# Rooms for gathered cache rows and window keys in a pool that is opened earlier, and the first of them requested beside the prompt's attention

## The chip, the cores and the metric

The kernel runs on one core of one Trainium2 chip. The metric is the device time of one execution in microseconds. Three runs of the kernel before took 1896.36, 1897.3 and 1900.26 us; the median is 1897.3 us.

## The reference, cut to what matters

One step of a hybrid decoder is computed for a prompt group (1 x 1024 tokens) and a sample group (8 sequences x 4 new tokens, each with 2048 cached positions in pages, and 512 rows of window state). Both share all weights. In float32:

```
h = rms_norm(x, g_attn); q, kc, vc, ks, vs, kw, vw, gates, ... = split(h @ w_in)
kcmp, vcmp = compress(kc), compress(vc)     # gelu(flat(32 rows + pe) @ w1) @ w2, stride 16
pc = softmax(q kcmp + bias);  o_cmp = pc vcmp
imp = pc @ sel_map;  idx = top 16 of the 64-row blocks (first, current and previous always in)
o_slc = softmax(q ks[idx] + bias) vs[idx]
o_win = softmax(q kw + bias over the last 512) vw
a = g0 o_cmp + g1 o_slc + g2 o_win
x = x + (sig(ga) (a @ w_nsa_out) + sig(gb) (conv @ w_conv_out)) @ w_o;  x = x + relu(norm(x) @ w_up)^2 @ w_down
```

For the sample group kc, vc, ks and vs are the cached pages, found by a page table, followed by the new rows, and kw and vw are the window state followed by the new rows. The step also returns the window state moved on by four rows (s_wk, s_wv).

## The kernel before, in words

The kernel is unrolled Python for a tile framework. The author writes tiles, pools and instructions; a list scheduler that runs against a planned timeline (schedule_with_timeline_sim) then fixes the order on each engine and each queue. An instruction that is written earlier has the better priority; tc.high_priority lifts what is written in it by 500 places; issue_after(x) puts what follows behind x on its engine. A tile whose room was another tile's waits for that tile's last use. Pools are opened on the left or the right end of the memory, as a stack on each side. All matmuls on wide data are done in three passes of high and low halves (mm3, L214 to L216).

The stages in order: RMSNorm and projections; the conv mixer's inputs; gates, with the prompt's attention beside them (stages(), driven by keep_pace and advance, at high priority); the conv output (pool conv); the sample group; merge; MLP.

Around the change:
- At the end of the conv output the pools gt and unit are opened on the right. gt holds GB = 2 rooms gth of 8 KB a partition: the compression's raw cache rows of one sequence, gathered by POOL (gather, L640).
- Four single units (sample_unit, i = 0 to ATTEND = 3) compress the cached keys of sequences 0 to 3 while the rest of the prompt's attention runs: compress(...), then advance(STEP[i]). Then advance(100) writes what is left of the attention, the pools unit, pa (the attention's, with its output tile ot) and cTh are closed, and s1, u2 and w2 are opened, with new PSUM banks (SMP).
- From there pairs of sequences are compressed (pair_unit, i = 4, 6, ... 14: two pairs of keys, four of values, in three products n = 0, 1, 2). The product n = 0 uses summed weights w2 (printed w), eight tiles of 256 KB that load_w2 loads on SP (L494). After each product the loop takes SSTEP = 3, 3, 4 steps of probs.
- probs = sample_group() is a generator: the sample group's own attention, step by step. weights(grp) transposes the window keys of four sequences (tiles swn, SWB = 2 rooms of 2 KB, loaded on SP at L1155), stores the moved window state from them (keep_window, L1103 and L1104), forms logits (sn, sw), the choice of blocks (L1206 with the constant lt, loaded at L1123), and the logits over the gathered selection rows (tiles gk, GK = 4 rooms of 4 KB, gathered by POOL at L633, 512 KB each; transposed at L1129). values(grp) multiplies by gathered value rows (so, L1113). fetch() asks for the next of 32 gathers whenever a room was used.
- In the kernel before, the rooms gk and swn are in s1. Two next(probs) are written right after s1 is opened: they write the first four gathers, lt, the first two key loads and their stores. load_w2 follows, its last four loads put behind the second key load.
- SP's queue carries, in order, the attention's stores (L990), lt, two key loads, then w.

Of the kernel before, what the change touches and what calls it, by code (L numbers as in the profile page):

```python
# [11 lines left out]
F32 = mybir.dt.float32  # L12
# [29 lines left out]
SWB = 2  # L42
# [34 lines left out]
GK = 4  # L77
# [43 lines left out]
def tile_hybrid_step(ctx, tc, xp, xs, cck, ccv, csk, csv, swk, swv, sconv, ptab, g_attn, w_in,  # L121
# [33 lines left out]
    def f32(ap):  # L155
        return ap.bitcast(F32)
# [261 lines left out]
    for j in range(4):  # L418
# [8 lines left out]
        h = j // 2  # L427
# [55 lines left out]
                P.dma_start(w2_d[sums, lp], f32(z).rearrange("p x c -> p (x c)"))  # L483
        return out

    def load_w2(kv, behind=None):

        out = {}
        for lp in range(8):
            z = w2p.tile([128, 2, 256], F32R, name="w2", tag="w2", bufs=8)  # L490
            with ExitStack() as e:
                if behind is not None and lp >= 4:
                    e.enter_context(tc.issue_after(behind.ins))
                DMA.dma_start(f32(z).rearrange("p x c -> p (x c)"), w2_d[kv, lp])  # L494
            out[16 + lp] = (z[:, 0], z[:, 1])
        return out

    HT = dict(ct="tp", hid="hd")

# [128 lines left out]

    def gather_half(cache, b, q):

        g = s1.tile([128, 1024], F32, name="gk", tag="gk", bufs=GK)
        rows = cache[0].rearrange("n (c q l) h d -> (n c q) (l h d)", q=2, l=8)
        P.indirect_dma_start(out=g, out_offset=None, in_=rows,  # L633
                             in_offset=bass.IndirectOffsetOnAxis(ap=idx2[:, q, b:b + 1], axis=0))
        return g
# [479 lines left out]
                    e.enter_context(tc.issue_after(ins.ins))  # L1115

    new_rows = {}
    nat_in = []

    def sample_group():  # L1120

        lt = s1.tile([128, 900], BF16, name="lt", bufs=1)
        DMA.dma_start(lt, lt_in.to_broadcast([128, 900]))  # L1123
        qb = [qbd[:, b].rearrange("p h g t -> p (h g t)") for b in range(NB)]
# [9 lines left out]
        def window_values(pw, rows, bs, ow):  # L1134
            pt = flipped([pw[:, i * 128:(i + 1) * 128] for i in range(4)], S.copy)
            po3 = ps(HT["sx"], "sv")
            for j0 in (0, 2):
                nats = {}
                for j in (j0, j0 + 1):
                    nats[j] = s1.tile([128, 4, 128], F32, name="swn", tag="swn", bufs=SWB)  # L1140
                    DMA.dma_start(nats[j], swv[0, bs[j]].rearrange("(k p) h d -> p k (h d)", p=128))
                    keep_window(s_wv[0, bs[j]], nats[j])
                in_turn([(po3[rows[j], :128], pt[:, i * 128 + 32 * j:i * 128 + 32 * j + 32], nats[j][:, i, :], i == 0, i == 3)
                         for i in range(4) for j in (j0 + 1, j0)])
            V.tensor_copy(ow, po3[:, :128])

        def weights(grp):
# [3 lines left out]
            bs = [grp * 4 + j for j in range(4)]  # L1151
            kts = []
            for b in bs:
                nat = s1.tile([128, 4, 128], F32, name="swn", tag="swn", bufs=SWB)
                nat_in.append(DMA.dma_start(nat, swk[0, b].rearrange("(k p) h d -> p k (h d)", p=128)))  # L1155
                keep_window(s_wk[0, b], nat)
                kts.append(flipped([nat[:, k, :] for k in range(4)], S.copy))
                yield
            while ("k", bs[-1]) not in have:
# [89 lines left out]
        def values(grp, ow):  # L1249
            rows = [slice(32 * j, 32 * j + 32) for j in range(4)]  # L1250
            bs = [grp * 4 + j for j in range(4)]
            def weights_T(q, n):
                pl = s1.tile([128, 512], F32, name="skt", tag="skt", bufs=SKT)
                DMA.dma_start(pl[:, :n], sl_d[grp, q, :, :n])
                return pl

            for half in range(2):
                pl = [weights_T(2 * half + i, 512) for i in range(2)]
                oo = ps(HT["sx"], "so")
                for j0 in (0, 2):  # L1260
                    gs = {j: gathered.pop(0) for j in (j0, j0 + 1)}
                    in_turn([(oo[rows[j], :128], pl[i // 4][:, i % 4 * 128 + 32 * j:i % 4 * 128 + 32 * j + 32],
                              gs[j][:, i * 128:(i + 1) * 128], i == 0, i == 7) for i in range(8) for j in (j0 + 1, j0)])
                    for _ in gs:
                        fetch()
                    yield
                V.tensor_add(ow, ow, oo[:, :128])
            pl = weights_T(4, 256)
            vn = s1.tile([128, 4, 128], F32, name="vn", tag="swn", bufs=SWB)[:8]
            DMA.dma_start(vn[:4], s_sv[0, bs[0]:bs[0] + 4].rearrange("b t h d -> t b (h d)"))  # L1270
            DMA.dma_start(vn[4:], s_wv[0, bs[0]:bs[0] + 4, WIN - ST:].rearrange("b t h d -> t b (h d)"))
            while ("v", bs[-1]) not in have:
                yield
            oo = ps(HT["sx"], "so")
            back = list(enumerate(bs))[::-1]
            in_turn([(oo[rows[j], :128], pl[:127, rows[j]], vcN[:, b, :], True, False) for j, b in back] +
                    [(oo[rows[j], :128], pl[:8, 128 + 32 * j:160 + 32 * j], vn[:, j, :], False, True) for j, b in back])
            V.tensor_add(ow, ow, oo[:, :128])
            yield
            own = s1.tile([128, 2, 64], F32, name="own", tag="mx")  # L1280
            V.tensor_scalar(own[:, 0], ow[:, 0:64], cst[:, K_M0:K_M0 + 1], None, op0=OP.mult)
            V.scalar_tensor_tensor(own[:, 0], ow[:, 64:128], cst[:, K_M1:K_M1 + 1], own[:, 0], op0=OP.mult, op1=OP.add)
            V.tensor_copy(own[:, 1], own[:, 0])
            pt = ps(HT["sk"], "ownT")
            PE.transpose(pt[:, :128], own.rearrange("p e d -> p (e d)"), ident)
            ts = mp.tile([128, 4, 16], F32, name=f"ts{grp}")
            for e in range(2):
                ro_ = slice(e * 64, e * 64 + 64)
                V.tensor_copy(ts[ro_].rearrange("p k (b t) -> p k b t", t=4),
                              pt[ro_, :128].rearrange("p (b k e t) -> p e k b t", b=4, k=4, e=2)[:, e])  # L1290
            new_rows[grp] = ts
            yield

        wanted = [(c, grp * 4 + j, half) for c in (csk, csv) for grp in range(2) for half in range(2) for j in range(4)]
        gathered = []

        def fetch():
            if wanted:
                gathered.append(gather_half(*wanted.pop(0)))

        for _ in range(GK):
            fetch()
        ows = []
        for grp in range(2):
            ows.append((yield from weights(grp)))
# [54 lines left out]
    def load_aT(qi):  # L1360
# [3 lines left out]
        for k in range(0, 4, 2):  # L1364
            S.copy(aTh[:, k:k + 2, s], at[:, k:k + 2])
            V.tensor_sub(aTl[:, k:k + 2, s], at[:, k:k + 2], f32(aTh[:, k:k + 2, s]))

    for i in range(ATTEND + 1):
        compress(sample_unit("k", cck, i, w1), ("k", i))
        advance(STEP[i])  # L1370
# [5 lines left out]
    w2p = open_pool("w2", "right")  # L1376
    HT.update(ct="ct", hid="hid", sk="sk", sx="sx")
    open_psum(**SMP)
    for _ in range(2):
        next(probs)  # L1380

    w1.update(load_w2(0, nat_in[-1]))
    for i in range(ATTEND + 1, 2 * NB, 2):
        if i == NB:
            w2 = load_w2(1)
            w1 = load_w1(w1v, W1B) | w2
        kv, cache = (("k", cck), ("v", ccv))[i // NB]
        unit = pair_unit(kv, cache, i % NB, w1)
# [530 lines left out]
```

## Time and profile before

| | |
|---|---|
| median of 3 runs | 1897.3 us (1896.36 to 1900.26) |
| profiled execution, own time | 1900.52 us |
| its span, first to last instruction | 1898.7 us |
| mean granted TensorE clock | 0.986 of full speed |
| busy: PE, PEld, DVE | 97%, 91%, 60% |
| busy: ACT, POOL | 46%, 25% |
| DMA, mean over the span | 163 GB/s |

The profile is one execution on the chip. PE is TensorE's matmuls, PEld its weight loads, DVE is VectorE, ACT ScalarE, POOL GpSimd, SPq the queue of SyncE, which issues most DMAs. Lxxx is a line of the kernel before. out<-in are the program's names for tiles. In brackets stands the time for which the engine had nothing just before, and what ended that wait. A clock of 1.00 is 2.4 GHz, 0.50 is 1.2 GHz.

### The profile page before, as it was taken

The numbers are of one execution on the slowest core, as the hardware profiler recorded it, in microseconds if no ns is written. First come the engines' busy times: TensorE is split into PE (matmuls) and PEld (weight loads), VectorE is DVE, ScalarE is ACT, GpSimd is POOL, SyncE is SP. The second block draws the span as 40 slices with busy tenths as digits, with TensorE's granted clock in tenths as the row PEclk, the third lists the DMA queues.
The fourth block names the chain that finished last, engine by engine and source line by source line (L and its number), as shares of the span: only waits on it lengthen the run. The fifth ranks groups of instructions, "written<-read, shape, count | busy, mean of one in ns | idle before, by whom it ended". The sixth has DMA issues, their size and how long they took to land.

```text
span 1898.7 us, 34944 instructions
## 1 busy us (share of the span) xinstructions
PE 1838.9 (97%) x13124; PEld 1734.0 (91%) x13124; DVE 1130.0 (60%) x2367; ACT 877.0 (46%) x1947; POOL 474.0 (25%) x710
## 2 busy tenths in 40 slices
PE   9999999999999999979999999999999999999998
PEld 7999999999998989858889887889999999999998
DVE  6324532444445676648777643697667646767765
ACT  5213322655555555656766212554545444544343
POOL 3213323445344443433332420131111100000000
PEclk9999999999999999989999999999999999999999
DMA  6457525322225531145757743546756567855664
GB/s 211 128 149 167 168 67 144 100 67 72 62 67 175 190 136 54 49 154 190 237 180 254 261 141 129 150 136 234 245 191 210 205 219 244 262 186 165 185 200 150
DMA packets 234202, 310.08 MB, mean 163 GB/s; under 512 B 21110, under 2 KB 162055, under 8 KB 229937
## 3 DMA queue, kind: packets, MB, share of 16 engines
q1 hardware_dynamic: 218416, 236.00, 40.5%
q0 software_dynamic: 15616, 71.84, 10.7%
q8 instruction: 104, 1.70, 0.4%
q14 instruction: 66, 0.53, 0.1%
HBM read 224.88 MB, written 82.90 MB: 162 GB/s over the span
## 4 chain that ended last, share of the span: by engine, by line
PE 83%; DMA 6%; DVE 4%; issue 3%; ACT 2%; POOL 2%; SPq 1%; POOLq 0%; DVEq 0%; ACTq 0%
PE c L215 10%; PE c L214 10%; PE c L216 10%; PE PT L957 3%; PE ga L215 3%; PE ga L214 3%; PE ga L216 3%; PE pv L964 2%; PE hid L215 2%; PE hid L216 2%; PE hid L214 2%; PE pv L963 2%; PE qkv L216 1%; PE qkv L215 1%; PE qkv L214 1%
## 5 line engine op out<-in xcount | busy, mean ns | idle before, releaser
L214 PE MATMUL c<-ud,whd 128*128 128x264 f32 x768 | 217.4, 286 | 5.5 <-ACT whd L1704 4.4
L215 PE MATMUL c<-ud,whd 128*128 128x264 f32 x768 | 218.4, 286 | 0.0
L216 PE MATMUL c<-ud,whd 128*128 128x264 f32 x768 | 215.6, 285 | 0.0
L883 POOL TENSOR_SCALAR P<-P,st,gates 128x256 f32<-128x256 f32 (+4 forms) x272 | 150.2, 568 | 115.9 <-DVE st L879 84.6
L214 PEld LDWEIGHTS c<-ud,whd 128*128 128x128 f32 x768 | 145.1, 190 | 6.1 <-ACT whd L1704 4.9
L214 PE MATMUL c<-hBt,wuh 128*128 128x264 f32 x512 | 145.9, 285 | 3.0 <-ACT p L1590 3.0
L216 PE MATMUL c<-hBt,wul 128*128 128x264 f32 x512 | 146.1, 285 | 0.0
L215 PEld LDWEIGHTS c<-ud,whd 128*128 128x128 f32 x768 | 145.4, 189 | 0.0
L216 PEld LDWEIGHTS c<-ud,whd 128*128 128x128 f32 x768 | 143.7, 189 | 0.0
L961 DVE TENSOR_TENSOR ptl<-PT,pth 128x512 fp32r<-128x512 f32 (+1 forms) x148 | 99.5, 685 | 64.1 <-ACT pth L960 63.6
L1704 ACT CAST whd<-wrd 128x512 fp32r<-128x512 f32 x112 | 68.2, 621 | 130.8 <-issue 97.8
L214 PE MATMUL ga<-hTh,whu 128*128 128x384 f32 (+1 forms) x384 | 127.7, 333 | 0.0
L215 PE MATMUL ga<-hTl,whu 128*128 128x384 f32 (+1 forms) x384 | 126.3, 329 | 0.0
L216 PE MATMUL ga<-hTh,wlu 128*128 128x384 f32 (+1 forms) x384 | 125.9, 328 | 0.0
L237 POOL TENSOR_TENSOR wlu<-wru,whu 128x1024 fp32r<-128x1024 f32 x32 | 76.7, 2398 | 154.1 <-ACT whu L236 154.0
L1705 DVE TENSOR_TENSOR whd<-wrd,whd 128x512 fp32r<-128x512 f32 x112 | 76.0, 689 | 64.3 <-ACT whd L1704 64.3
L960 ACT CAST pth<-PT 128x512 fp32r<-128x512 f32 (+1 forms) x148 | 83.7, 588 | 61.0 <-PE PT L957 57.5
L215 PE MATMUL c<-h2r,wuh 128*128 128x264 f32 x384 | 109.8, 286 | 1.4 <-POOL h2r L1616 0.8
L957 PE MATMUL PT<-cst,P 128*128 128x128 f32 (+1 forms) x592 | 101.8, 277 | 0.2 <-DVE st L938 0.2
L214 PEld LDWEIGHTS c<-hBt,wuh 128*128 128x128 f32 x512 | 97.2, 190 | 3.2 <-ACT p L1590 3.2
L216 PEld LDWEIGHTS c<-hBt,wul 128*128 128x128 f32 x512 | 96.9, 189 | 0.0
L1625 POOL DMA_DIRECT2D u_d<-u x64 | 34.7, 543 | 248.7 <-ACT u L1623 240.8
(554 smaller groups left out, 5977.9 us busy)
## 6 DMA issues: line engine op xcount, KB each, us to landing
ur<-u_d SPq DMA_DIRECT2D x96, 264.0 KB
wru<-in_w_up SPq DMA_DIRECT2D x36, 512.0 KB
u_d<-u POOLq DMA_DIRECT2D x64, 264.0 KB, 3.8
wru<-in_w_in SPq DMA_DIRECT2D x32, 512.0 KB
wrd<-sd_d SPq DMA_DIRECT2D x64, 256.0 KB
h2r<-in_w_down SPq DMA_DIRECT2D x28, 512.0 KB
sd_d<-h2r POOLq DMA_DIRECT2D x14, 1024.0 KB, 5.3
wrd<-in_w_down SPq DMA_DIRECT2D x48, 256.0 KB
```

Source lines behind the costliest of these rows:

```text
L214: PE.matmul(out, wh, ah, start=first, stop=False)
L215: PE.matmul(out, wh, al, start=False, stop=False)
L216: PE.matmul(out, wl, ah, start=False, stop=last)
L237: (leng or P.tensor_sub)(l, raw, f32(h))
L883: P.tensor_scalar(p, p, self.st[:, br, 3, g:g + 1], gates[:, self.qi, 3 * hg + br:3 * hg + br + 1], op0=OP.mult, op1=OP.mult)
L957: PE.transpose(pt[:n, g * 128:(g + 1) * 128], pg[g], ident)
L960: S.copy(hi[:n], pt[:n])
L961: V.tensor_sub(lo[:n], pt[:n], f32(hi[:n]))
L963: PE.matmul(self.o, w, hi[:n], start=first and i == 0, stop=False)
L964: PE.matmul(self.o, w, lo[:n], start=False, stop=last and i == len(tiles) - 1)
L1704: S.copy(h, raw)
L1705: lows.append(V.tensor_sub(l, raw, f32(h)))
```

## The change

Three things change. The tiles gk, swn and vn are taken from gt in place of s1. The generator has a new first part, which writes the four first gathers and the first two key loads with their stores, and then yields; it is run once, before the four single units. The two steps behind the opening of s1 are dropped, load_w2 has no loads held back, and key loads written after it stand behind its last load. lt is now written at the first step inside the unit loop.

```diff
-    def load_w2(kv, behind=None):
+    def load_w2(kv):
...
-            with ExitStack() as e:
-                if behind is not None and lp >= 4:
-                    e.enter_context(tc.issue_after(behind.ins))
-                DMA.dma_start(f32(z).rearrange("p x c -> p (x c)"), w2_d[kv, lp])
+            ins = DMA.dma_start(f32(z).rearrange("p x c -> p (x c)"), w2_d[kv, lp])
             out[16 + lp] = (z[:, 0], z[:, 1])
-        return out
+        return out, ins
...
     def gather_half(cache, b, q):
-        g = s1.tile([128, 1024], F32, name="gk", tag="gk", bufs=GK)
+        g = gt.tile([128, 1024], F32, name="gk", tag="gk", bufs=GK)
...
+        def keys(b):
+            nat = gt.tile([128, 4, 128], F32, name="swn", tag="swn", bufs=SWB)
+            with ExitStack() as e:
+                if w2_in:
+                    e.enter_context(tc.issue_after(w2_in[0].ins))
+                DMA.dma_start(nat, swk[0, b].rearrange("(k p) h d -> p k (h d)", p=128))
+            keep_window(s_wk[0, b], nat)
+            return nat
+
+        for _ in range(GK):
+            fetch()
+        early = [keys(b) for b in range(SWB)]
+        yield
         lt = s1.tile([128, 900], BF16, name="lt", bufs=1)
         DMA.dma_start(lt, lt_in.to_broadcast([128, 900]))
...
-                    nats[j] = s1.tile([128, 4, 128], F32, name="swn", tag="swn", bufs=SWB)
+                    nats[j] = gt.tile([128, 4, 128], F32, name="swn", tag="swn", bufs=SWB)
...
-                nat = s1.tile([128, 4, 128], F32, name="swn", tag="swn", bufs=SWB)
-                nat_in.append(DMA.dma_start(nat, swk[0, b].rearrange("(k p) h d -> p k (h d)", p=128)))
-                keep_window(s_wk[0, b], nat)
+                nat = early.pop(0) if early else keys(b)
...
-        for _ in range(GK):
-            fetch()
         ows = []
...
+    next(probs)
     for i in range(ATTEND + 1):
         compress(sample_unit("k", cck, i, w1), ("k", i))
         advance(STEP[i])
...
-    for _ in range(2):
-        next(probs)
-
-    w1.update(load_w2(0, nat_in[-1]))
+    w2, ins = load_w2(0)
+    w1.update(w2)
+    w2_in.append(ins)
```

(wanted, gathered and fetch move up with the gathers; vn is taken from gt as well.)

## Rows read from the trace of the kernel before

**Rows 1.** Page, part 1: busy us of each engine (share of the span), instructions.

```profile
PE 1838.9 (97%) x13124; PEld 1734.0 (91%) x13124; DVE 1130.0 (60%) x2367; ACT 877.0 (46%) x1947; POOL 474.0 (25%) x710
```

**Rows 2.** PE in order of time at the hand-over: start, us, what [wait, releaser].

```profile
829.08 0.50 PE L964 MATMUL pv<-ptl,pvc 64*128 64x512 f32 x1
831.80 1.86 PE L674 MATMUL ct<-cst,gpr 128*128 128x128 f32 x8 [2.23 <-DVE gpr L653]
841.50 2.02 PE L1129 MATMUL skT<-cst,swn 128*128 128x128 f32 x8 [7.83 <-DMA swn<-in_state_win_k]
...
844.02 0.56 PE L214 MATMUL hid<-cth,w 128*128 128x256 f32 x1
```

**Rows 3.** Windows of 2 us: length, busy PE PEld DVE ACT POOL, PEclk, DMA, GB/s.

```profile
832.00:834.00 2.00, 1.66 (x8) 1.26 (x7) 0.08 (x1) 0.89 (x2) 0.87 (x2) 0.50 0.91 326
...
844.00:846.00 2.00, 2.00 (x13) 2.00 (x12) 0.00 (x0) 1.24 (x3) 0.00 (x0) 0.59 0.89 286
```

**Rows 4.** SP's queue in order of time at the hand-over: start, us, issue.

```profile
830.46 1.43 SPq L990 DMA_DIRECT2D aT_d<-ot  x2
836.27 0.34 SPq L1123 DMA_DIRECT2D lt<-in_lt  x1
836.66 0.98 SPq L1155 DMA_DIRECT2D swn<-in_state_win_k  x2
837.68 1.64 SPq L494 DMA_DIRECT2D w<-w_d  x3
```

**Rows 5.** Waits of SP's queue, 780 to 900: total us, times, longest.

```profile
SPq L1123 <- DMA aT_d<-ot: 4.2, 2, 4.0
```

**Rows 6.** POOL in order of time, at gt's opening and at the hand-over.

```profile
699.83 1.07 POOL L640 DMA_INDIRECT gth<-in_cache_cmp_k,idx  x1 [0.90 <-DVE ptl L961]
...
704.26 6.91 POOL L883 TENSOR_SCALAR P<-P,st,gates 128x384 f32<-128x384 f32 x12 [1.71 <-DVE st L879]
...
825.51 0.98 POOL L633 DMA_INDIRECT gk<-in_cache_slc_k,idx  x1 [0.16 <-issue]
```

**Rows 7.** VectorE in order of time at the hand-over.

```profile
835.08 0.69 DVE L697 TENSOR_TENSOR ctl<-xt,cth 128x512 fp32r<-128x512 f32 x1
```

**Rows 8.** Windows of 2 us around the second half's gathers.

```profile
880.00:882.00 2.00, 0.83 (x5) 0.61 (x5) 1.97 (x2) 1.99 (x4) 1.70 (x2) 1.00 0.92 334
882.00:884.00 2.00, 0.91 (x9) 0.42 (x8) 2.00 (x6) 2.00 (x5) 1.39 (x3) 0.79 1.03 311
884.00:886.00 2.00, 0.74 (x5) 0.77 (x5) 1.12 (x3) 0.23 (x1) 0.76 (x1) 0.50 1.02 397
```

**Rows 9.** POOL's groups of instructions, 690 to 832: busy us, mean ns.

```profile
L640 POOL DMA_INDIRECT gth<-in_cache_cmp_k,idx x6 | 6.0, 1002 | 2.7 <-DVE ptl L961 1.6 <-POOL gpr L649 0.8 <-DVE st L879 0.3
...
L633 POOL DMA_INDIRECT gk<-in_cache_slc_k,idx x4 | 3.8, 958 | 1.1 <-issue 1.1
```

**Rows 10.** Windows of 4 us where the compression of the sample group begins.

```profile
700.00:704.00 4.00, 2.89 (x16) 2.01 (x13) 3.84 (x17) 2.61 (x10) 1.89 (x2) 1.00 0.65 210
704.00:708.00 4.00, 2.83 (x18) 2.21 (x18) 2.55 (x10) 2.04 (x8) 3.73 (x6) 1.00 0.96 391
```

**Rows 11.** The tile gth: its gathers of values, ns min/median/max.

```profile
L640 POOL DMA_INDIRECT gth<-in_cache_cmp_v,idx x8: 938/1032/1957, 873.7 to 985.7; - x8
```

**Rows 12.** PE in order of time later: last early key transposes, end of the units.

```profile
863.55 0.60 PE L1129 MATMUL skT<-cst,swn 128*128 128x128 f32 x4
...
1051.07 1.16 PE L531 MATMUL kvc<-w2v,gx 128*127 128x64 f32 x8 [0.86 <-DVE gx L507]
...
1066.60 1.94 PE L1113 MATMUL so<-gk,skt 128*32 128x128 f32 x32 [1.20 <-DMA gk<-in_cache_slc_v,idx]
...
1071.27 1.08 PE L214 MATMUL na<-aTh,wnh 128*128 128x288 f32 x3 [0.83 <-ACT aTh L1424]
```

**Rows 13.** POOL in order of time at the end of the sample group.

```profile
1057.62 0.94 POOL L633 DMA_INDIRECT gk<-in_cache_slc_v,idx  x1 [0.30 <-issue]
```

**Rows 14.** The tile gk: idle us before its instructions by releaser, times.

```profile
  PE so L1113: 29.7, 6
```

More of the change, by code (lines that the diff above doesn't have):

```diff
@@ L1117, in tile_hybrid_step, with fetch @@
     new_rows = {}
-    nat_in = []
+    w2_in = []
     def sample_group():
+        wanted = [(c, grp * 4 + j, half) for c in (csk, csv) for grp in range(2) for half in range(2) for j in range(4)]
+        gathered = []
+        def fetch():
+            if wanted:
+                gathered.append(gather_half(*wanted.pop(0)))
+        def keys(b):
[10 more added lines that the diff above has]
+        yield
         lt = s1.tile([128, 900], BF16, name="lt", bufs=1)
@@ L1268, in values @@
             pl = weights_T(4, 256)
-            vn = s1.tile([128, 4, 128], F32, name="vn", tag="swn", bufs=SWB)[:8]
+            vn = gt.tile([128, 4, 128], F32, name="vn", tag="swn", bufs=SWB)[:8]
             DMA.dma_start(vn[:4], s_sv[0, bs[0]:bs[0] + 4].rearrange("b t h d -> t b (h d)"))
@@ L1292, in values @@
             yield
[L1294 to L1299, printed above, removed]
-        for _ in range(GK):
-            fetch()
         ows = []
@@ L1378, in tile_hybrid_step @@
     open_psum(**SMP)
-    for _ in range(2):
-        next(probs)
-    w1.update(load_w2(0, nat_in[-1]))
+    w2, ins = load_w2(0)
+    w1.update(w2)
+    w2_in.append(ins)
     for i in range(ATTEND + 1, 2 * NB, 2):
         if i == NB:
-            w2 = load_w2(1)
+            w2, _ = load_w2(1)
             w1 = load_w1(w1v, W1B) | w2
```

## The prediction

> **What bounds the kernel now.** I read the page's shares first: PE is busy 97% of the span [rows 1], so the whole kernel has some 60 us in which PE waits, and only work that is in PE's way counts. The reader should then go to the stretch that the change touches, the hand-over from the prompt's attention to the sample group. PE's own instructions in order of time [rows 2] show it: the last attention matmul starts at 829.08; eight transposes of compression rows follow after 2.23 us of waiting; then PE stands 7.83 us until 841.50, and what ends that wait is the load of a key row (swn); the first product with the summed weights (hid from w) starts at 844.02. The clock rows [rows 3] add the second half of the cost: the granted clock is 0.50 from 832 on and still 0.59 as a mean over 844 to 846, so the lower of its two levels (1.2 GHz) holds until about 845.6, after an engine that had nothing for 10 us.
>
> Why is the key row late? SP's queue [rows 4] answers: two stores of the attention's output at 830.46, then nothing until lt at 836.27, then two key loads at 836.66, then w. The waits of that queue [rows 5] say that lt stood up to 4.0 us for the landing of aT_d from ot. Everything behind lt stood with it. The gathered rows (gk), which the change also moves, were asked for at 825.51 [rows 6], when POOL had finished the last scaling of P; they are not what PE waits for here.
>
> **The change part by part.**
>
> *The key rows.* Two loads and their four keep_window stores go from behind lt to a place beside the attention, with room in gt. That takes the 7.83 us wait away. What is late next is the pair unit itself: its first lower half ctl starts at 835.08 and takes 0.69 [rows 7], so hid cannot start before 835.77; and its first weight tile w. In the new program load_w2 stands ahead of lt (lt is now asked for in the loop), so I take w to be first on SP behind the two stores, which end at 830.46 + 1.43 = 831.89, and to be issued at about 832.2. The nearest row for its flight is the first key load, issued at 836.66 and used at 841.50: 4.84 us with lt (128 x 900 bf16) ahead of it. So w is there at 837.0, against 844.02 now: **7.0 us**. The eight key transposes (2.02 us even at the low clock) fit into the 3.3 us between 833.7 and 837.0. Ends: 8.2 us if w comes earlier and ctl decides (844.02 less 835.77); 2.5 us if lt still stands ahead and w is issued at 836.66 as the keys were (844.02 less 841.5). I take 7.0, by the row of the same queue and size. "DMA: Bandwidth & Descriptors" of the Trainium skill, in its anatomy of one DMA, fits a transfer as 2.0 us plus its bytes at 436 GB/s; that estimate is 2.6 us for 256 KB, and by it w would land at 834.8 and the term would be 8.2. That fit is for GpSimd's path; the row, on SP's queue, is nearly twice as long.
>
> *The clock.* From 841.50 to about 845.6 PE works at half rate, which costs 4.1 / 2 = 2.1 us. In the new kernel PE still has 2.2 us without work before 831.8 and some 1 to 3 us before hid. Ends: 0 and 2.1 gained. I take 0: at 882 to 884 the clock fell with only about half of the stretch idle [rows 8].
>
> *The four gathers.* Each is one POOL instruction of 958 ns, 0.3 us apart: some 5.0 us of POOL's queue for four [rows 6, 9]. They go from 825.5, where POOL had nothing else (gain 0), to the opening of gt, ahead of the compression's first gathers, now at 699.83 [rows 6]. These 1 MB gathers then start and land up to 5.0 us later, and the scaling of P at 704.26 stands behind them on POOL. There PE is already short of work: 2.89 and 2.83 us busy in two 4 us stretches [rows 10], 28% idle, since the attention alone does not fill it. Ends of the loss: 0 (the gathers fit into the 0.9 us holes and PE's order is planned around them) and 8.3 us, worked out below. I take 28% of 5.0 = **1.4 us lost**, by the row of that stretch.
>
> The six gathers that ran beside the attention took 1002 ns each, four in the emptier stretch 958 [rows 9]: 4 x 0.044 = 0.2 us, hidden by POOL's slack. "DMA: Bandwidth & Descriptors" of the Trainium skill, in SWDGE vs HWDGE vs iDMA, speaks against this part: GpSimd writes a gather's descriptors into SBUF, and VectorE locks it out while it runs in its two-port mode. The longest gather of this trace, 1957 ns beside a busy VectorE [rows 11], bounds what that could do: 4 x 1.0 = 4.0 us on POOL, of which 28% would be another 1.1 us. The trace bears the small value out.
>
> *SP's new work beside the attention.* Two loads and four stores at 0.5 us (two loads take 0.98) [rows 4] are some 3 us of a queue that otherwise carries q loads and output stores there; a store that waits for its key row can hold the queue for the 4.84 us of such a load, with a q load behind it. I cost it at nothing, since a q tile has two buffers; if that cover is gone, the price is at most 4.8 us once.
>
> *Moved steps.* The sample group gets two steps fewer before the unit loop. From the first hid at 844.02 [rows 2] to the last kvc at 1051.07 [rows 12] six units of ten steps take 207 us, 3.45 us a step, so its program order falls back by 6.9 us against the units. Against this its first group of keys is complete only at 863.55 [rows 12], since the third and fourth key loads wait for rooms and for SP; with the first two done early they can be issued right behind w, near 836, and be used near 842. I take these two as balanced, with a small gain at the end: the sample's last gather at 1057.62 [rows 13] makes PE wait 1.20 us at 1066.60 [rows 12]. A chain that starts earlier loses that wait: **1.2 us**. Ends: 0 and 2.0 (with the 0.83 at 1071.27).
>
> *Removed wait in load_w2.* The four late w loads no longer stand behind a key load; that is in the 7.0.
>
> Sum: 7.0 + 1.2 - 1.4 = **6.8 us less**. The profiled execution took 1900.5 us, its span 1898.7; the median of the runs is 1897.3, 3.2 lower, and I apply the difference to the median: **1890.5 us**. A run of this kernel tells about 0.2% (3.8 us) from no change.
>
> **The rivals.**
>
> *More than this.* From 880 to 886 PE is busy 0.83, 0.91 and 0.74 of 2 us each [rows 8], 3.5 us idle, waiting among others for the second half's gathers; a sample group that starts earlier asks for them earlier. With the 2.1 us of clock at the hand-over and the other 0.8 us of the tail that is 6.4 us more: 1884.1. For: the first key group can be done 15 to 20 us earlier. Against: those gathers need rooms that only the first half's transposes free, and VectorE is full in that stretch.
>
> *The gain is spent at the start.* If the planner puts the four gathers ahead of everything on POOL and the compression's rows are late in PE's fixed order, the loss at 700 to 712 is the whole 5.0 us plus the scaling of P pushed from 704.26 to 707.6, 3.3 us: 8.3 instead of 1.4. Then the sum is 0.1 worse than nothing: about 1897.4, no change. For: PE idles there already, DMA runs at 391 GB/s when those rows come in [rows 10]. Against: POOL has 0.9 us holes and much slack later. A variant with the same outcome is that the moved work stays where it was, the gathers behind POOL's last scaling and w behind lt: 2.5 us less, 1.4 lost.
>
> *Slower: the tail.* PE's spare work at the end (na) runs out just as the last gathered rows arrive: PE waits 1.20 and 0.83 us there [rows 12]. If the sample group's chain is held by its program order rather than by its waits, it ends 6.9 us later while the units end no earlier for the kernel, and each us beyond 1066.6 is a us of the total: 1897.3 + 6.9 = 1904.2. It decides from the point where the last gather is issued after 1061.4. Against: the gathers stood 29.7 us in six waits for rooms that the products so give free [rows 14], so it is rooms and flights that hold the chain now, and those come with an earlier start.
>
> **How the numbers follow.** The forecast gets 0.50, its own range 1886 to 1894 (from both ends of the clock, w and the tail, and a start that costs between 0 and 5.0). More than this 0.18; spent at the start 0.19; the tail 0.13. The range 1880 to 1899 takes in the first three, with 4 us below the first rival for terms that add up, and leaves out the tail. Faster by over 0.2%: 0.50 + 0.18 = 0.68; within 0.2%: 0.19; slower: 0.13. The likeliest is the forecast, 1890.5.
>
> **What would show it.** Right: in the changed profile PE's wait for swn near 834 is gone; SP shows w directly behind the last two aT_d stores and lt behind w; hid from w starts 6 to 8 us after the last attention matmul, not 15; the gathers of gk stand near 700 on POOL. Wrong: w issued after lt, or hid starting more than 12 us after the attention; PE waits for ct from gth between 700 and 715 that add up to over 5 us; a last gk gather that is not at least 4 us earlier than 1057.62.

## The result, and the profile after

The changed kernel takes 1915.3 us (median of 5 runs, 1909.4 to 1921.8) against 1897.3: a ratio of **1.0084** (95% interval 1.0062 to 1.0105), some 16 us slower. A second measurement on another chip gave 1.0070 (1.0052 to 1.0087). The profiled execution took 1913.6 us; its span is 1911.8, 13.2 more than before.

The shares of the page stand as they stood [rows 1]:

```profile
PE 1846.3 (97%) x13124; PEld 1738.4 (91%) x13124; DVE 1130.3 (59%) x2367; ACT 878.2 (46%) x1947; POOL 475.0 (25%) x710
```

So I cut the span at instructions of PE that both kernels have: in the last product of the conv output, at the last attention matmul, at the first hid from w, at that of the first pair of values, in the last na; the fifth window goes on to the end. The windows, kernel before (columns as in rows 3; the number behind x counts the engine's instructions in the window):

```profile
696.11:829.08 132.97, 127.47 (x870) 109.22 (x868) 92.63 (x259) 80.64 (x224) 58.02 (x102) 1.00 0.19 64
829.08:844.02 14.94, 4.88 (x23) 3.98 (x22) 2.99 (x6) 3.64 (x7) 2.76 (x10) 0.60 0.77 236
844.02:911.13 67.11, 62.84 (x525) 55.89 (x523) 50.69 (x92) 41.95 (x83) 21.84 (x24) 0.94 0.64 211
911.13:1106.13 195.00, 183.52 (x1596) 169.54 (x1595) 144.75 (x261) 103.42 (x198) 70.86 (x70) 0.98 0.68 226
1106.13:1898.65 792.52, 772.68 (x5941) 749.52 (x5939) 514.21 (x821) 345.47 (x626) 74.52 (x130) 0.99 0.59 192
```

The changed kernel:

```profile
696.80:833.37 136.57, 129.27 (x869) 112.02 (x868) 92.42 (x259) 81.08 (x224) 58.28 (x110) 0.96 0.24 81
833.37:840.38 7.01, 4.03 (x30) 3.05 (x29) 2.31 (x6) 4.50 (x10) 1.21 (x2) 1.00 0.48 148
840.38:917.62 77.24, 68.64 (x563) 57.31 (x563) 54.68 (x103) 45.44 (x87) 26.56 (x26) 0.96 0.64 209
917.62:1117.18 199.56, 184.23 (x1548) 170.23 (x1547) 141.69 (x253) 99.67 (x191) 67.00 (x69) 0.96 0.63 209
1117.18:1911.84 794.66, 774.14 (x5941) 750.96 (x5939) 514.42 (x819) 345.40 (x625) 75.93 (x130) 0.99 0.58 192
```

The lengths differ by +3.6, **-7.9**, **+10.1**, +4.6 and +2.1 us. The hand-over's wait is gone; the rest gives back more than twice as much. The third and fourth windows are best read together: after the change the third holds 563 of PE's instructions in place of 525, and the fourth 48 fewer, so a part of the +10.1 is work that moved (32 products with window values, sv, among it). Length less PE's busy time is idle time: in the first four windows 31.3 us before and 34.2 after. The other 7.5 us are busy time, for as many instructions (3010 and 3014). The cause that the rows show for a part of it is the clock: it is 0.96 at the start, where it was 1.00, and 0.96 among the values, where it was 0.98. (The last window, +2.1, and the 0.7 before the first hold none of the changed work: by so much two executions differ.)

PE at the hand-over, answering [rows 2]:

```profile
833.37 0.40 PE L961 MATMUL pv<-ptl,pvc 64*128 64x512 f32 x1
835.58 1.06 PE L1149 MATMUL skT<-cst,swn 128*128 128x128 f32 x8 [1.81 <-issue]
...
840.38 0.38 PE L214 MATMUL hid<-cth,w 128*128 128x256 f32 x1
...
848.01 1.08 PE L1149 MATMUL skT<-cst,swn 128*128 128x128 f32 x4 [2.57 <-DMA swn<-in_state_win_k]
```

SP's queue beside it, answering [rows 4]:

```profile
834.65 1.43 SPq L987 DMA_DIRECT2D aT_d<-ot  x2
836.52 3.67 SPq L491 DMA_DIRECT2D w<-w_d  x8
840.24 0.43 SPq L1143 DMA_DIRECT2D lt<-in_lt  x1
840.76 0.94 SPq L1133 DMA_DIRECT2D swn<-in_state_win_k  x2
```

The first two key rows are there, w is directly behind the stores and hid starts 7.0 us after the attention in place of 14.9. The **third key row** stands behind eight loads of w and lt: issued at 840.76, used at 848.01. PE waits 2.57 us for it in the middle of the first pair's product n = 0. In the kernel before, that row stood behind w too, and PE did not wait for it; SP and PE there:

```profile
845.97 2.90 SPq L1155 DMA_DIRECT2D swn<-in_state_win_k  x2
```

```profile
856.55 0.60 PE L1129 MATMUL skT<-cst,swn 128*128 128x128 f32 x4
```

Its use stands 27.5 us behind the last attention matmul before, and 14.6 after: PE's new order asks for it 13 us sooner than the old one, and it comes a little later than that.

POOL at gt's opening, answering [rows 6]:

```profile
700.34 1.07 POOL L630 DMA_INDIRECT gk<-in_cache_slc_k,idx  x1 [0.72 <-issue]
...
704.25 0.94 POOL L630 DMA_INDIRECT gk<-in_cache_slc_k,idx  x1 [0.30 <-issue]
705.49 0.94 POOL L637 DMA_INDIRECT gth<-in_cache_cmp_k,idx  x1 [0.30 <-ACT P L871]
...
707.71 1.30 POOL L880 TENSOR_SCALAR P<-P,st,gates 128x384 f32<-128x384 f32 x2
```

And windows of 4 us there, answering [rows 10]:

```profile
704.00:708.00 4.00, 1.46 (x7) 0.87 (x6) 2.53 (x11) 1.51 (x6) 3.11 (x4) 1.00 0.98 325
708.00:712.00 4.00, 3.03 (x12) 2.65 (x12) 1.35 (x5) 1.23 (x4) 4.00 (x8) 0.52 1.04 411
712.00:716.00 4.00, 3.48 (x11) 2.24 (x10) 2.05 (x4) 1.98 (x5) 1.92 (x5) 0.50 1.01 411
716.00:720.00 4.00, 4.00 (x23) 3.63 (x22) 3.02 (x10) 3.19 (x10) 0.00 (x0) 0.70 0.16 49
```

The compression's first gather is issued at 705.49, not 699.83 (5.0 us later when counted from the start of the window). From 704 to 708 PE is busy 1.46 us where it was 2.83, and then the clock is 0.50 for some 10 us, though PE works most of them.

The longest new wait of PE is farther on, in the first pair of values:

```profile
932.51 0.58 PE L214 MATMUL hid<-cth,w 128*128 128x256 f32 x1 [4.40 <-ACT cth L693]
```

The waits of ScalarE there, kernel before (900 to 935) and changed kernel (905 to 940), in total us, times, longest:

```profile
ACT w1h L473 <- DMA w1r<-in_cmp_w_v: 6.1, 3, 2.6
```

```profile
ACT w1h L473 <- DMA w1r<-in_cmp_w_v: 10.7, 3, 6.1
```

Behind it on SP, in the changed kernel:

```profile
925.93 0.38 SPq L1100 DMA_DIRECT2D out<-swn  x1
926.36 0.61 SPq L471 DMA_DIRECT2D w1r<-in_cmp_w_v  x1
```

A load of value weights (w1r) is issued right behind a store of the moved window, which had waited 3.5 us for its key row. ScalarE, in order, stands 6.1 us for that load, with the pair's cth behind it, and PE stands for cth.

### The profile page after: what moved, and what is told of

Its sections match the earlier page's. It is cut to its first block, busy times and chain, and to the rows that moved or that the text cites. A ratio compares the mean times of both kernels' runs of the same rounds, so it can differ in the third digit from the quotient of the medians.

```text
span 1911.8 us, 34947 instructions
## 1 busy us (share of the span) xinstructions
PE 1846.3 (97%) x13124; PEld 1738.4 (91%) x13124; DVE 1130.3 (59%) x2367; ACT 878.2 (46%) x1947; POOL 475.0 (25%) x710
## 4 chain that ended last, share of the span: by engine, by line
PE 84%; DMA 6%; DVE 4%; issue 2%; ACT 2%; POOL 1%; SPq 1%; DVEq 0%; POOLq 0%; ACTq 0%
PE c L215 11%; PE c L214 11%; PE c L216 11%; PE PT L954 3%; PE ga L215 3%; PE ga L214 3%; PE ga L216 3%; PE hid L214 2%; PE hid L215 2%; PE hid L216 2%; PE pv L961 2%; PE pv L960 2%; DMA x_d<-xo 1%; PE qkv L216 1%; PE qkv L215 1%
## 5 line engine op out<-in xcount | busy, mean ns | idle before, releaser
L237 POOL TENSOR_TENSOR wlu<-wru,whu 128x1024 fp32r<-128x1024 f32 x32 | 76.7, 2398 | 157.3 <-ACT whu L236 157.2
```

The source lines that it names most:

```text
L237: (leng or P.tensor_sub)(l, raw, f32(h))
```

## The experiments

Ratios are to the kernel before, on the same chip, with their 95% intervals. "+" and "-" are against the changed kernel where nothing else is said.

### One part at a time

**e1**: rooms alone. gk, swn, vn in gt; gathers, key rows, lt, w and both steps written as in the kernel before.

> Tiles gk, swn and vn taken from gt as in the changed kernel, but everything written where the kernel before has it: a control. Theory 'keys' (the early key rows let the sample group run ahead of the units, and that is what costs some 15 us between 845 and 1180; the gathers alone cost about 4 us near 705): no change, 1897 within 3 us, last attention matmul at 829, hid from w at 844. Rival 'rooms' (which rooms the tiles have shifts the planned order, and the loss comes from that): over 1903. Rival 'gathers' (the loss comes from gathered rows that are there too early): 1897 here as well.

Measured: **0.9994** (0.9980 to 1.0009). But the hand-over is not where the kernel before has it. With the rooms free early, the planner asks early, wherever the lines stand; POOL and SP of this kernel:

```profile
703.74 0.94 POOL L633 DMA_INDIRECT gk<-in_cache_slc_k,idx  x1 [0.30 <-issue]
```

```profile
702.11 0.39 SPq L1137 DMA_DIRECT2D swn<-in_state_win_k  x1
703.10 0.72 SPq L1137 DMA_DIRECT2D swn<-in_state_win_k  x1
...
836.35 0.94 SPq L1137 DMA_DIRECT2D swn<-in_state_win_k  x2
837.54 0.35 SPq L1146 DMA_DIRECT2D lt<-in_lt  x1
837.93 5.63 SPq L494 DMA_DIRECT2D w<-w_d  x8
```

The first two key rows are asked for at 702 and 703, the third and fourth directly ahead of lt and w; lt no longer waits for a landing. hid starts 10.9 us after the attention. So early gathers, early key rows and an earlier hid come with the rooms alone, and cost nothing; "rooms" is out. Two things of the changed kernel are not in e1: the third key row behind w, and the order that comes of the dropped steps. (Its gathers also stand behind the compression's first two, not ahead of them.)

**e2**: only the gathers written early.

```diff
         for _ in range(GK):
             fetch()
-        early = [keys(b) for b in range(SWB)]
+        early = []
         yield
```

(and load_w2, its place and the two steps ahead of it as before)

> Only the four first gathers are written beside the attention; key rows, lt and w stay as in the kernel before. Theory 'keys': the start loses about 4 us (last attention matmul near 833, low clock after 708), nothing else: 1901, from 1899 to 1903; hid from w 15 us after the attention. Rival 'gathers': the middle loses as well, 1909 or more. Rival 'rooms': as the control.

Measured: 1.0013 (0.9998 to 1.0027), as "keys" had it; "gathers" (1909 or more) is out. But here too the planner asked for the first two key rows early, at 699.75 and 700.74, so this is not the gathers alone.

**e3**: only the key rows written early; gathers at the hand-over.

```diff
-        for _ in range(GK):
-            fetch()
         early = [keys(b) for b in range(SWB)]
         yield
+        for _ in range(GK):
+            fetch()
+        yield
```

(and one more step of probs ahead of load_w2, which runs the gathers)

> The two first key rows and their stores stay early, w is first on SP at the hand-over, but the four gathers are written at the hand-over as in the kernel before. Theory 'keys': last attention matmul near 829, hid from w near 836.5, then some 15 us lost between 845 and 1180: 1907 to 1913. Rival 'gathers': the hand-over's 8 us stay as a gain and nothing is lost behind: 1889 to 1892. Rival 'rooms': the control plus what the hand-over gives, 8 us less than the control.

Measured: 1.0033 (1.0019 to 1.0046), less than "keys" wanted; the planner moved the gathers early here too, to 700.65 and after. So none of e1 to e3 parts the gathers from the key rows.

**e4**: the two steps back, behind load_w2.

```diff
     w2_in.append(ins)
+    for _ in range(2):
+        next(probs)
```

> The changed kernel with two steps of the sample group written again ahead of the unit loop, behind the loads of w: its key transposes come back to the place in the order that they had before. If the two dropped steps are what cost (the planned order falls back against the units, as one of my rivals had it): 1903 to 1908. Theory 'keys' (the sample group already runs too far ahead): 1915 or more, up to 1920. If two steps of some seventy don't matter: 1915 within 3 us.

Measured: **1.0013** (0.9999 to 1.0027), some 11 to 13 us faster than the changed kernel. So with the two steps back most of the loss is gone, at least as much as "dropped steps" forecast. The reason that went with it, a sample group that falls back, does not fit, and "keys" is out: the second set of keys comes earlier still (921.2 against 924.8). The third key row stays behind w here, and PE waits longer for it than in the changed kernel:

```profile
851.31 1.12 PE L1149 MATMUL skT<-cst,swn 128*128 128x128 f32 x4 [3.92 <-DMA swn<-in_state_win_k]
```

### How many steps, and the gathers held

**e5, e6, e7**: 5, 7 or 1 steps behind the first product of the unit loop, where the changed kernel has 3; **e8**: the steps of e4, and the four gathers held on POOL:

```diff
+            with tc.issue_after(raw_in[-1].ins):
                 fetch()
```

(raw_in holds the gathers of gth; this part is run in the last single unit)

> The changed kernel, with the two dropped steps of the sample group given back inside the first pass of the unit loop (5 steps behind its product n = 0 in place of 3), not ahead of the loop. Theory 'behind' (two steps fewer by then put the sample group's priority behind the units for good, wherever they are lost): ratio to the kernel before 1.001, as with the steps ahead of the loop. Rival 'ahead of the first unit' (only their place before the first product matters): 1.008, as the changed kernel. Rival 'phase' (which step falls beside which product decides, earlier or later alike): between these or outside, with no order.

> As the run before, with 7 steps there: the sample group's order two steps ahead of the kernel before. 'Behind': 1.001 or lower, 0.997 if each step is worth what the first two were worth. 'Ahead of the first unit': 1.008. 'Phase': anything, above all over 1.004 would speak for it.

> As the changed kernel, with 1 step there in place of 3: two more steps behind. 'Behind': 1.012 to 1.016. 'Ahead of the first unit': 1.008. 'Phase': anything, below 1.006 would speak for it.

> The changed kernel with the two steps ahead of the unit loop and with the four gathers of selection rows held on POOL behind the last single unit's own gather (near 740 in place of 700). Theory 'start' (the four gathers ahead of the compression's own and of the scaling of P cost 3 to 4 us there, and nothing gives that back): ratio 0.999, last attention matmul some 129 us behind the first gather of the compression, not 133. Rival 'hidden' (what is lost at the start is given back at the hand-over, where PE waits anyway): 1.001 as with the steps alone.

Measured: five 1.0007 (0.9992 to 1.0022), seven 0.9999 (0.9988 to 1.0011), **one 1.0018** (1.0002 to 1.0033). Two steps more and two fewer both bring the loss back to 0 to 0.2%. "Behind" falls by e7, "ahead of the first unit" by all three; "phase" is left: that the 3 steps of the changed kernel are a bad pairing of the sample group's work with the pairs', not the end of a slope. That is argued; no run shows which pairing. All three keep the third key row behind w and wait 3.1 to 3.4 us for it and 1.7 to 4.8 for the fourth. e8: 1.0025 (1.0010 to 1.0039). The first window shortens by 0.9 us only (135.7), its clock is 0.99 in place of 0.96, and none of it is seen in the time: "start" is not confirmed.

### The third key row, and lt

**e9**: the changed kernel again. **e10**: without the hold on later key loads; **e11**: e10 with the steps of e4.

```diff
-                if w2_in:
-                    e.enter_context(tc.issue_after(w2_in[0].ins))
```

**e12**, against the kernel before: lt written behind `w1.update(load_w2(0, nat_in[-1]))`, nothing else.

> The changed kernel once more, beside the others of this call. All theories that explain the whole of its loss: 1.008. If the runs with one or seven first steps are the rule, and the first measurement was high: 1.002 to 1.005.

> The changed kernel without the hold that puts the third and fourth key row behind the last load of w. Theory 'third key row' (PE, freed of the wait for the first key row, waits for the third and fourth instead, whose loads stand behind 2 MB of w on SP: a wait in the place of the one removed): the wait for swn at 845 and after goes, idle time and low clock from the first hid to the fourth unit fall from 9.6 us to under 4, and the time by 5 to 6 us, to 1.005 if the changed kernel again gives 1.008. Rival 'units' (what comes late is the units, held by VectorE and ScalarE; the key rows only fill their gaps): no change against the changed kernel.

> Without that hold, and with the two steps ahead of the unit loop. 'Third key row': 11.4 us of idle time and low clock from the first hid to the fourth unit fall to under 4, so 0.997 to 0.998 against the kernel before (the steps alone gave 1.0013). 'Units': 1.001 as with the steps alone.

> The kernel before with one edit: lt is written behind the loads of w, so that the two first key rows stand directly behind the attention's last stores on SP. If the hand-over's wait comes from lt in front of the key rows: they are issued near 832.2, hid from w starts some 10 to 11 us behind the last attention matmul instead of 14.9, and the time falls by 4 us, ratio 0.998. If the key rows wait for the same room as lt did: no change, 1.000.

Measured: e9 1.0070 (1.0052 to 1.0087). **e10 1.0013** (1.0001 to 1.0025): without the hold the changed kernel is 11 to 13 us faster. SP and the third window of e10:

```profile
836.10 0.40 SPq L1130 DMA_DIRECT2D swn<-in_state_win_k  x1
836.56 3.80 SPq L491 DMA_DIRECT2D w<-w_d  x8
```

```profile
841.38:907.40 66.02, 61.78 (x538) 53.34 (x536) 50.99 (x94) 40.61 (x77) 24.51 (x23) 0.99 0.67 223
```

The third key row is asked for ahead of w, and the two pairs of keys take 66.0 us in place of 77.2 (with 25 instructions fewer). "Units" had no change here, and fails. But e11 is 1.0014 (0.9999 to 1.0030), as "units" had it and not as "third key row" had: the two cures do not add up. The four runs make a square:

| | steps dropped | steps back |
|---|---|---|
| hold on later key loads | 1.0084, 1.0070 (after, e9) | 1.0013 (e4) |
| no hold | 1.0013 (e10) | 1.0014 (e11) |

The loss stands in one corner only. The third key row behind w costs 11 to 13 us together with the dropped steps, and nothing that these runs can tell without them; so the wait for that row, 2.57 us here and 3.92 in e4, is not what these microseconds are.

e12 is the bare form of the change's idea, with one line moved. hid starts 8.1 us after the attention, not 14.9, the start is untouched (132.5 us), and yet it is **1.0029** (1.0013 to 1.0045), slower than the kernel before, which neither expectation had. Its pairs of keys take 76.0 us; lt and w stand ahead of the third key row, which is issued and used as late as before (855.76 against 856.55) though hid starts 8.5 us sooner:

```profile
840.67 0.57 SPq L1382 DMA_DIRECT2D lt<-in_lt  x1
844.87 1.00 SPq L1153 DMA_DIRECT2D swn<-in_state_win_k  x2
```

### The value weights

**e13**: `with tc.high_priority():` around `load_w1(w1v, W1B)`. **e14**: both stores of keep_window on POOL's queue (`P.dma_start`). **e17**: in load_w1, for the value weights only:

```diff
-            S.copy(h, raw)
-            V.tensor_sub(l, raw, f32(h))
+            (split or S.copy)(h, raw)
+            (P if split else V).tensor_sub(l, raw, f32(h))
```

(split is P.tensor_copy there)

> The changed kernel, with the loads and the splitting of the value weights (w1r, w1h, w1l) written at high priority: on SP two of the eight loads move ahead of stores of the window, the rest of the queue stays. Theory 'weights behind stores' (the sample group's second set of window keys now falls beside the loading of the value weights; its stores wait on SP for key rows, a load of w1r stands behind them, ScalarE waits 6 us for it with a cth behind, and PE waits 4.4 us for that cth): that wait of PE goes and the changed kernel's ratio of 1.007 to 1.008 falls to 1.002 to 1.005. Rival 'no one place' (the order as a whole got worse, and any nudge shakes it): no way to tell the size, but the waits near 928 would stay as they are and the ratio too, 1.006 to 1.008.

> The changed kernel with all stores of the moved window state issued on POOL's queue in place of SP's. 'Weights behind stores': nothing on SP waits for a window key row any more, 1.001 to 1.005. Rival 'no one place': 1.006 to 1.008. If the stores hold POOL instead, gathers come late and the time is above 1.008.

> The changed kernel, with the splitting of the value weights (w1h and w1l from w1r) on GpSimd in place of ScalarE and VectorE; every order up to the second pair of keys stays. Theory 'held queue' (ScalarE's order puts splits of weights that are still on their way in front of the pairs' cth, so PE, freed at the hand-over, waits there instead; the first pair of values is where the gain goes): PE's wait for cth near 928 (4.4 us) goes and no like one comes, ratio 1.002 to 1.005. Rival 'no one place': 1.006 to 1.009, with new waits of the same sum elsewhere between 910 and 1070. If GpSimd, held by the same loads, delays gathers: above 1.009.

Measured: e13 1.0056 (1.0032 to 1.0079), e14 1.0050 (1.0031 to 1.0068), **e17 1.0016** (1.0005 to 1.0027). In e13 the wait for cth is 1.90 us in place of 4.40, in e14 1.36. The gain is of that size, 3 to 6 us, but both intervals overlap with those of the changed kernel. e17 takes the standing away as a whole. Its pairs of keys are as slow as the changed kernel's (76.8 us), its fourth window is 13 us shorter, for as many instructions (1549 and 1548), with the clock at 0.99:

```profile
919.63:1106.30 186.67, 179.85 (x1549) 166.13 (x1548) 143.77 (x248) 97.36 (x188) 79.23 (x79) 0.99 0.68 226
```

(that execution is the shortest of its 12 runs, so some 5 us of the 13 may be its luck). So "held queue" stands as one condition of the loss: without the splits on ScalarE and VectorE the changed kernel is 10 to 13 us faster. It is not the only one, since e4 and e10 keep the splits and are as fast.

### A version that keeps each gain

**e15**: e1, with lt behind w and the gathers held on POOL as in e8. **e16**: that with keep_window on POOL. **e18**: e15 with the split of e17.

> The control with rooms in gt, with lt written behind w, and with the four gathers held on POOL behind the last single unit's gather. By the terms one by one (the start unharmed, third and fourth key rows directly behind the attention's stores, w behind them): 5 to 7 us less than the kernel before, 0.996 to 0.9975. Rival 'given back' (every earlier hid so far was followed by as much waiting in the two pairs of keys, so the hand-over's wait was no loss to begin with): 0.999 to 1.002.

> As the run before, with the stores of the window state on POOL's queue as well. By the terms: 0.995 to 0.997. 'Given back': 0.999 to 1.002.

> The same edit on the kernel with rooms in gt, lt behind w and held gathers, whose one long wait after the hand-over is 7.2 us for cth behind such a split, at 915. 'Held queue': that wait goes, and 5 to 7 us with it: 0.9955 to 0.9965 against the kernel before, faster by more than the measurement's doubt. 'No one place' or 'given back': 0.998 to 1.001.

Measured: e15 **0.9989** (0.9973 to 1.0006), e16 1.0077 (1.0058 to 1.0096), e18 1.0001 (0.9988 to 1.0014). e15 is the fastest of all, but no more than level with the kernel before. Its one long wait after the hand-over is at the value weights again, though that load was issued in good time, at 909.76, beside two gathers of 1 MB; ScalarE and PE:

```profile
919.82 0.62 ACT L473 CAST w1h<-w1r 128x512 fp32r<-128x512 f32 x1 [7.33 <-DMA w1r<-in_cmp_w_v]
```

```profile
922.09 0.58 PE L214 MATMUL hid<-cth,w 128*128 128x256 f32 x1 [7.17 <-ACT cth L698]
```

e18 takes exactly that wait away, and the time does not fall: other waits come later (3.1 us for gx until 958, 2.2 for a window value row until 987, 1.4 and 2.3 for ctl until 995 and 1002). In e16 the stores hold POOL: at 715 POOL stands 5.8 us for a key row, and PE then 3.8 us for P, which POOL scales; at 935 PE waits 6.9 us for a key row.

The lengths of the first four windows, one execution each:

| kernel | start | hand-over | pairs of keys | values to na | sum | ratio |
|---|---|---|---|---|---|---|
| before | 133.0 | 14.9 | 67.1 | 195.0 | 410.0 | 1 |
| after | 136.6 | 7.0 | 77.2 | 199.6 | 420.4 | 1.0084 |
| e9 after again | 136.4 | 7.0 | 80.5 | 196.7 | 420.6 | 1.0070 |
| e1 rooms | 135.6 | 10.9 | 67.4 | 192.2 | 406.2 | 0.9994 |
| e4 steps back | 136.6 | 6.5 | 76.7 | 188.4 | 408.2 | 1.0013 |
| e10 no hold | 135.5 | 8.4 | 66.0 | 201.7 | 411.7 | 1.0013 |
| e12 lt last | 132.5 | 8.1 | 76.0 | 196.7 | 413.3 | 1.0029 |
| e15 | 134.0 | 8.6 | 64.9 | 199.4 | 406.9 | 0.9989 |
| e17 split | 135.3 | 7.0 | 76.8 | 186.7 | 405.8 | 1.0016 |

after and e9 are one kernel: single windows differ by 3 us between two executions of it, the sums by 0.2. And an execution can lie off its median: that of before was 3.2 us longer than the median of its runs, that of e17 5.2 us shorter.

The pairs of keys do not hold equal work either (525 instructions of PE before, 503 in e7, 538 in e10). In the runs where they hold 554 to 567, they take 67 to 70 us where the third key row is asked for ahead of w (e1, e2, e11, e16), and 74 to 82 where it stands behind w (after, e9, e3 to e6, e8, e12 to e14, e17). So that row's place does set the length of this window. But it does not set the time: in the slow group e5 has 1.0007, e6 0.9999 and e17 1.0016, in the fast group e2 1.0013 and e16 1.0077. What was lost in the pairs of keys can be made up among the values, and the other way round.

## Why the prediction was wrong, step by step

Every sign that I had named for being right came: PE's wait is gone, w is behind the stores, lt behind w, hid starts 7.0 us after the attention, the gathers stand near 700. Of the signs of being wrong none came (the last gather is 10 us earlier, at 1047.62). All of them look at the hand-over, at the start or at the sample group's chain, and none at the pairs that follow.

**The key rows, 7.0 forecast: right.** The hand-over is 7.9 us shorter. w is issued 3.1 us behind the last attention matmul, where I put it, lt behind it, and the eight key transposes fit in.

**The clock, 0 forecast: up to some 4 us lost.** The 0.60 of the hand-over became 1.00, but the low level came back elsewhere. At the start it held for some 10 us. What that costs can be read from kernels with the same two waits of PE there: with some 10 us at 0.50 the window is 136.2 to 136.6 us (after, e9 and six more), with 7 us 135.3 and 135.5 (e17, e10), with 3 us 135.0 (e11; e14 is left aside, since its stores hold POOL there). So it is some 2 us, an estimate from these lengths. Among the values PE worked 13.9 us at 0.50 in place of 6.4; half of the 7.5 us more, some 4, is the most that this can cost. The hand-over gave back 2. I had bounded the term by the gain that it had held, 0 to 2.1; that it could be lost at other places I did not price.

**The four gathers, 1.4 forecast with 0 to 8.3 as ends: 3.6 in length, not theirs alone.** The window holds the same work (870 and 869 instructions of PE), 1.8 us more of it idle. The gathers did what the second rival said: all four stand ahead of the compression's own, which come 5 us later, and the scaling of P is at 707.71. But with the gathers held until 748 (e8) the window is still 135.7, 0.9 less than in e4, from which e8 differs by that hold. With early rooms and gathers behind the compression's first (e1) it is 135.6, in e15 134.0, without early rooms (before, e12) 133.0 and 132.5. So the gathers' place is worth some 1 us by e8, the clock that falls behind them included; what the rest is stays open.

**GpSimd's descriptors, 0.2 forecast: 0.1.** The four gathers took 0.94 to 1.07 us each beside the attention, 0.985 as a mean. The lock-out by VectorE that "DMA: Bandwidth & Descriptors" of the Trainium skill describes (SWDGE vs HWDGE vs iDMA) does not show on these four.

**SP's new work, 0 forecast: right as far as seen.** A store stood 4.8 us on SP for its key row, as I had feared, and no wait of PE at the start is for a q load.

**Moved steps, "balanced", then 1.2 gained: the step that failed.** I took the 7.0 us of the hand-over as a gain of the whole kernel, and the two dropped steps as made up for by the earlier key rows. The two windows behind the hand-over lost 14.7 us in place of gaining 1.2, and e4, which only puts the two steps back, is 11 to 13 us faster. My times were not what failed: the third key row was issued 7.4 us behind the last attention matmul (forecast: 6.9) and used 14.6 behind it (12.9). What I left out is that PE's order behind the hand-over is planned anew. It asks for that row 13 us sooner than before, so that 2.57 us of waiting (3.31 and 3.28 for two rows in e9) come in the place of the wait removed; and in the first pair of values it stands 4.40 us for a cth behind value weights that are still on their way. These two waits are 7.0 of the 14.7. Neither alone is the loss, since it goes when either the hold (e10), the dropped steps (e4) or the splits (e17) are taken back.

**The tail.** My slow rival had the sign and not the mechanism. The sample group did not fall back; its last gathered products start earlier than in [rows 12] and wait for nothing:

```profile
1060.63 1.94 PE L1110 MATMUL so<-gk,skt 128*32 128x128 f32 x32
```

The pairs end late: their last kvc starts at 1073.0 in place of 1051.07 [rows 12], and at 1062.1 in e17.

**What stays open.** The 8 us of the hand-over come out in no version. e1 and e15 end level with the kernel before, with 4.0 and 6.3 us less in the second window; in e1 the last gather is asked for 30 us earlier as well. No single wait holds the rest: when one was taken away (e11, e18), others of its size came. Behind the hand-over PE, VectorE and ScalarE are busy 94, 74 and 53% of the fourth window of the kernel before, in orders that are fixed beforehand and wait for each other; that PE's standing at the hand-over is therefore no pure loss is my reading, argued and not shown. Nor is it shown why three different edits (e4, e10, e17) each win back 10 to 13 us, and two of them together (e11) no more. That any change of the planned order does as well is not so: e13 and e14 won back 3 to 6.

## What to carry to other kernels

When a wait is taken away, look at what the new order asks for sooner: a load that came in comfort (here the third key row) may now be late, and it is priced with all bytes issued ahead of it, not alone. Signs of being right belong behind the place that is changed, too: here all signs at the place itself came true and the kernel got slower. Where several engines run nearly full in orders planned beforehand, a gain at one place is worth something only if the profile behind it shows the same work ending earlier; a 7 us wait removed gave between -2 and +16 us here. One edit that cures a loss does not show its cause: turn each suspect back alone and together, as in the square above, before a wait is called the reason. And a room that is free early can move a transfer by itself, wherever its line is written.

## What was not expected of the hardware

- PE's clock fell to 0.50 behind short waits, not only behind long ones: after waits of 1.46 and 2.05 us (704 to 709) it stayed there for some 10 us, while PE worked most of the time; it fell again behind the 2.57 us until 848 (0.57 as a mean from 848 to 852) and in the 4.40 us until 932.5 (0.50 from 930 to 934). In the kernel before it is 1.00 from 696 to 829, with one wait of 1.45 us at the same place. It is not the waits alone: behind the same two waits the low level held for some 7 us in e10 and e17 and 3 us in e11, and in e1, with waits of 1.46 and 1.82 us there, the clock is 1.00 all along the start.
- At the start, where PE also waits for others, the low clock cost less than half of the time that it held: 7 us less of it (e11 against the changed kernel) made that window 1.5 us shorter.
- Key rows of 256 KB took 4.8 us from issue to use behind lt, 7.2 us behind 2 MB of w; in e15 a load of value weights of 256 KB, issued beside two gathers of 1 MB, was used 10 us after its issue and kept ScalarE standing 7.33 us.
- The same kernel's runs lie up to 0.9% apart (e13: 1904.1 to 1921.9), so one profile says little on differences under 5 us; the ratios above rest on 5 to 12 runs of each changed version.
